# Loading w in pairs of k tiles and storing the last column group in two DMAs: a 64-row window matmul on one core

## The chip, the cores and the metric

One core of a Trainium2 chip runs the whole program. The metric is device time in microseconds (us): the median over several executions. The span that a trace shows, from its first to its last instruction, is 1.6 to 1.7 us shorter than the time of the same execution (184.73 against 183.1 before), so differences of spans can be read as differences of time.

## The reference

For each of four batches, 64 consecutive rows of x, from an offset known only at run time, are multiplied by the same w.

```python
B, S, D, W = 4, 4096, 4096, 64
for b in range(B):
    o = int(offsets[b])
    results.append(x[b, o:o+W] @ w)      # (64 x 4096) @ (4096 x 4096), fp32
```

w is 64 MB of fp32 and is used once. x contributes 4 MB, the output is another 4 MB. What counts is how fast w comes in.

## The kernel before

The PE (TensorE) does the matmuls; it adds up its results in banks of PSUM, from which ScalarE and VectorE copy them. Two batches share a tile of 128 rows (G = 2 such tiles). The columns are worked in two groups of 2048 (NG), the k dimension in 32 tiles of 128. Eight PSUM banks hold one column group for both row tiles. A load reads one k tile of one column group, 128 rows of 8 KB (1 MB of fp32), and the DMA casts it to fp16. Only the last k tile of the last group is loaded in four parts, so that its matmuls, copies and stores can follow each other in small steps.

```python
wh_pool = ctx.enter_context(tc.tile_pool(name="wh", bufs=24))
sth_pool = ctx.enter_context(tc.tile_pool(name="sth", bufs=8))
# ... (other pools, the first k tile through ScalarE's queue) ...
def load(ng, ki):
    t = wh_pool.tile([P, NG], fp16, name="wh", tag="wh")
    nc.gpsimd.dma_start(
        out=t[:], in_=w[ki * P : (ki + 1) * P, ng * NG : (ng + 1) * NG])
    return t[:]
# ... (x loaded and transposed) ...
for ng in range(n_ng):
    for ki in range(n_k):
        # ...
        if ng == n_ng - 1 and ki == n_k - 1:
            for j in range(n_sub):                  # four parts of 512 columns
                # ... wl{j} <- 128 rows of 2 KB
        else:
            wh[(ng, ki)] = load(ng, ki)
# ... (matmuls; group 0 is copied to stage[g]) ...
for g in range(G):                                  # group 0: two stores of 1 MB
    nc.gpsimd.dma_start(out=out[2*g : 2*g+2, :, 0:NG], in_=stage[g][:])
ki = n_k - 1
q = [nc.scalar, nc.sync]
for j in range(n_sub):                              # group 1: eight stores of 256 KB
    cs = (n_ng - 1) * NG + j * NT
    for g in range(G):
        mm(g, j, ki, wlast[j][:], False, True)
        s = sth_pool.tile([P, NT], fp32, name="sth", tag="sth")
        # ... copy bank -> s, ScalarE for g == 0, VectorE for g == 1
        q[g].dma_start(out=out[2*g : 2*g+2, :, cs : cs + NT], in_=s[:])
```

In this program a DMA issued from GpSimd gets one of eight semaphores in turn; so does a DMA issued from ScalarE or SyncE, from eight others. A semaphore is a counter that the DMA raises when it has landed. A DMA waits until the one eight places before it has landed.

Of the kernel before, what the change touches and what calls it, by code (L numbers as in the profile page):

```python
# [1 line left out]

# [5 lines left out]


@with_exitstack  # L10
def kernel(
    ctx: ExitStack,
    tc: tile.TileContext,
    x: bass.AP,
    w: bass.AP,
    offsets: bass.AP,
    out: bass.AP,
):
    nc = tc.nc
    fp32 = mybir.dt.float32  # L20
    fp16 = mybir.dt.float16

    B, S, D = x.shape
    _, N = w.shape
    WIN = out.shape[1]
    P = 128
    NT = 512
    NG = 2048
    n_k = D // P
    n_ng = N // NG  # L30
    n_sub = NG // NT
    G = B // 2

    POOL = mybir.EngineType.Pool

    const_pool = ctx.enter_context(tc.tile_pool(name="const", bufs=1))
    x_pool = ctx.enter_context(tc.tile_pool(name="xp", bufs=1))
    wh_pool = ctx.enter_context(tc.tile_pool(name="wh", bufs=24))
    wl_pool = ctx.enter_context(tc.tile_pool(name="wl", bufs=1))
    st_pool = ctx.enter_context(tc.tile_pool(name="st", bufs=1))  # L40
    sth_pool = ctx.enter_context(tc.tile_pool(name="sth", bufs=8))
    psum_pool = ctx.enter_context(tc.tile_pool(name="ps", bufs=1, space=bass.MemoryType.PSUM))

    identity = const_pool.tile([P, P], fp16, name="identity")
    off_t = const_pool.tile([1, B], mybir.dt.int64, name="off_t")
    w0_32 = x_pool.tile([P, N], fp32, name="w0row")
    w0_16 = x_pool.tile([P, N], fp16, name="w0half")
    x16 = [x_pool.tile([P, D], fp16, name=f"xrow{g}") for g in range(G)]
    xT = [x_pool.tile([P, D], fp16, name=f"xT{g}") for g in range(G)]
    ps = [psum_pool.tile([P, NT], fp32, name=f"bank{t}") for t in range(8)]  # L50

    ctx.enter_context(tc.manual_schedule())

    nc.sync.dma_start(out=off_t[:], in_=offsets[None, :])
    nc.scalar.dma_start(out=w0_32[:], in_=w[0:P, :])
    off_i32 = off_t.bitcast(mybir.dt.int32)

    def load(ng, ki):
        t = wh_pool.tile([P, NG], fp16, name="wh", tag="wh")
        nc.gpsimd.dma_start(  # L60
            out=t[:], in_=w[ki * P : (ki + 1) * P, ng * NG : (ng + 1) * NG]
        )
        return t[:]

    wh = {(ng, 0): w0_16[:, ng * NG : (ng + 1) * NG] for ng in range(n_ng)}
    wh[(0, 1)] = load(0, 1)
    make_identity(nc, identity[:])
    for b in range(B):
        g, m = divmod(b, 2)
        o = nc.values_load(  # L70
            off_i32[0:1, 2 * b : 2 * b + 1],
            engines=[POOL],
            min_val=0,
            max_val=S - WIN,
            skip_runtime_bounds_check_because="offsets are drawn below S - WIN",
        )
        nc.gpsimd.dma_start(  # L77
            out=x16[g][m * WIN : (m + 1) * WIN, :],
            in_=x[b][bass.ds(o, WIN), :]
        )  # L80
    wlast = []
    for ng in range(n_ng):
        for ki in range(n_k):
            if (ng, ki) in wh:
                continue
            if ng == n_ng - 1 and ki == n_k - 1:
                for j in range(n_sub):
                    cs = ng * NG + j * NT
                    t = wl_pool.tile([P, NT], fp16, name=f"wl{j}")
                    nc.gpsimd.dma_start(  # L90
                        out=t[:], in_=w[ki * P : (ki + 1) * P, cs : cs + NT]
                    )
                    wlast.append(t)
            else:
                wh[(ng, ki)] = load(ng, ki)

    nc.scalar.copy(out=w0_16[:, :NG], in_=w0_32[:, :NG])  # L97
    nc.scalar.copy(out=w0_16[:, NG:], in_=w0_32[:, NG:])  # L98
    for g in range(G):
        for t in range(8):  # L100
            for i in range(4):
                k = 4 * t + i
                nc.tensor.matmul(  # L103
                    out=ps[t][:, i * P : (i + 1) * P],
                    lhsT=x16[g][:, k * P : (k + 1) * P],
                    rhs=identity[:],
                    start=True,
                    stop=True,
                )
            dst = xT[g][:, t * NT : (t + 1) * NT]  # L110
            if t % 2 == 0:
                nc.vector.tensor_copy(out=dst, in_=ps[t][:])  # L112
            else:
                nc.scalar.copy(out=dst, in_=ps[t][:])  # L114

    def mm(g, j, ki, rhs, start, stop):
        nc.tensor.matmul(  # L117
            out=ps[4 * g + j][:],
            lhsT=xT[g][:, ki * P : (ki + 1) * P],
            rhs=rhs,  # L120
            start=start,
            stop=stop,
        )

    stage = [st_pool.tile([P, NG], fp32, name=f"stage{g}") for g in range(G)]
    for ng in range(n_ng):
        last = ng == n_ng - 1
        for ki in range(n_k - 1 if last else n_k):
            for g in range(G):
                for j in range(n_sub):  # L130
                    mm(g, j, ki, wh[(ng, ki)][:, j * NT : (j + 1) * NT], ki == 0, ki == n_k - 1)
        if not last:
            for j in range(n_sub):
                for g in range(G):
                    dst = stage[g][:, j * NT : (j + 1) * NT]
                    if g == 0:
                        nc.scalar.copy(out=dst, in_=ps[4 * g + j][:])  # L137
                    else:
                        nc.vector.tensor_copy(out=dst, in_=ps[4 * g + j][:])  # L139
    for g in range(G):  # L140
        nc.gpsimd.dma_start(out=out[2 * g : 2 * g + 2, :, 0:NG], in_=stage[g][:])  # L141
    ki = n_k - 1
    q = [nc.scalar, nc.sync]
    for j in range(n_sub):
        cs = (n_ng - 1) * NG + j * NT
        for g in range(G):
            mm(g, j, ki, wlast[j][:], False, True)
            s = sth_pool.tile([P, NT], fp32, name="sth", tag="sth")
            if g == 0:
                nc.scalar.copy(out=s[:], in_=ps[4 * g + j][:])  # L150
            else:
                nc.vector.tensor_copy(out=s[:], in_=ps[4 * g + j][:])  # L152
            q[g].dma_start(out=out[2 * g : 2 * g + 2, :, cs : cs + NT], in_=s[:])  # L153


# [1 line left out]
_INS = ['x', 'w', 'offsets']  # L157
_OUTS = [((4, 64, 4096), 'float32')]


# [23 lines left out]
```

## Time and profile before

| | before |
|---|---|
| time | 184.98 us (184.97 to 185.01, 3 runs) |
| span of the trace | 183.1 us |
| PE busy | 126.3 us (69%) |
| GpSimd busy | 38.3 us (21%) |
| DMA engines | full from slice 1 to slice 38 of 40 |

Lines from the page of the kernel before. In the first two, each of 40 entries is a slice of 4.58 us: the busy share of the 16 DMA engines in tenths, and what they moved (GB/s as written, so a casting load counts half of what it reads). Then come the packet counts, the queue of the GpSimd DMAs, the chain of waits by line, the two groups that matter (busy us, mean ns, idle us before it and its main cause), and DMA issues (KB each, median us from issue to landing).

```profile
DMA  6999999999999999999999999999999999999994
GB/s 179 348 221 215 207 213 215 215 214 211 213 211 214 215 213 214 214 216 214 211 214 212 213 213 214 213 215 214 215 213 212 213 214 212 213 213 205 387 403 172
DMA packets 11271, 40.97 MB, mean 224 GB/s; under 512 B 1282, under 2 KB 1794, under 8 KB 10626
...
q0 software_dynamic: 9968, 36.70, 97.0%
...
DMA wh<-in_w_dram 90%; ACT sth L150 1%; PE bank L117 1%; ACTq L153 1%; POOLq L60 0%; POOLq L168 0%
...
L117 PE MATMUL bank<-wh,xT 128*128 128x512 f16 x488 | 113.8, 378 | 28.6 <-DMA wh<-in_w_dram 28.6
...
L60 POOL DMA_DIRECT2D wh<-in_w_dram x61 | 32.4, 531 | 112.5 <-DMA wh<-in_w_dram 100.2
...
wh<-in_w_dram POOLq DMA_DIRECT2D x61, 512.0 KB, 19.1
...
out_dram<-sth ACTq DMA_DIRECT2D x4, 256.0 KB, 6.5
out_dram<-sth SPq DMA_DIRECT2D x4, 256.0 KB, 6.6
```

The DMA row and the chain agree: the kernel is a stream of DMA work, and the PE waits for tiles. 19.1 us from issue to landing is not the length of one load. It is the length of a queue of eight.

The end of the time line of the kernel before (start us, us, engine, line, what, and in brackets the idle time before it and what ended it):

```profile
166.48 1.89 PE L117 MATMUL bank<-wh,xT 128*128 128x512 f16 x8 [0.52 <-DMA wh<-in_w_dram]
...
168.93 1.89 PE L117 MATMUL bank<-wh,xT 128*128 128x512 f16 x8 [0.57 <-DMA wh<-in_w_dram]
...
170.65 1.89 PE L117 MATMUL bank<-wl,xT 128*128 128x512 f16 x8
171.07 0.58 ACT L150 COPY sth<-bank 128x512 f32<-128x512 f32 x1 [73.36 <-PE bank L117]
...
171.69 0.34 ACTq L153 DMA_DIRECT2D out_dram<-sth  x1
172.01 2.12 SPq L153 DMA_DIRECT2D out_dram<-sth  x4
```

A k tile is used every 2.45 us and costs the PE 1.89 us. The DMA's share and rate in windows of that end (the numbers at the end of each line are the granted PE clock, DMA share, GB/s):

```profile
169.00:171.00 2.00, 2.00 (x10) 0.90 (x10) 0.00 (x0) 0.00 (x0) 0.00 (x0) 1.00 1.23 297
...
173.00:175.00 2.00, 0.00 (x0) 0.00 (x0) 0.77 (x2) 1.17 (x2) 0.00 (x0) 0.97 1.01 426
...
177.00:179.00 2.00, 0.00 (x0) 0.00 (x0) 0.00 (x0) 0.00 (x0) 0.00 (x0) 0.50 1.06 410
179.00:181.00 2.00, 0.00 (x0) 0.00 (x0) 0.00 (x0) 0.00 (x0) 0.00 (x0) 0.50 0.75 287
```

The DMA engines stay full until 179 us and more, long after the last matmul: 4 MB of stores follow the loads.

### The profile page before, as it was taken

The numbers are of one execution on the slowest core, as the hardware profiler recorded it, in microseconds if no ns is written. First come the engines' busy times: TensorE is split into PE (matmuls) and PEld (weight loads), VectorE is DVE, ScalarE is ACT, GpSimd is POOL, SyncE is SP. The second block draws the span as 40 slices with busy tenths as digits, with TensorE's granted clock in tenths as the row PEclk, the third lists the DMA queues.
The fourth block names the chain that finished last, engine by engine and source line by source line (L and its number), as shares of the span: only waits on it lengthen the run. The fifth ranks groups of instructions, "written<-read, shape, count | busy, mean of one in ns | idle before, by whom it ended". The sixth has DMA issues, their size and how long they took to land.

```text
span 183.1 us, 1380 instructions
## 1 busy us (share of the span) xinstructions
PE 126.3 (69%) x576; PEld 56.4 (31%) x576; DVE 10.5 (6%) x16; ACT 14.1 (8%) x19; POOL 38.3 (21%) x77
## 2 busy tenths in 40 slices
PE   0004799988877777887779878777777877777600
PEld 0004664433333233333324333323232333333200
DVE  0002530000000000000005000000000000000500
ACT  2081430000000000000013000000000000000310
POOL 4612221222222112222221222222122222210000
PEclk9999999999999999999999999999999999999965
DMA  6999999999999999999999999999999999999994
GB/s 179 348 221 215 207 213 215 215 214 211 213 211 214 215 213 214 214 216 214 211 214 212 213 213 214 213 215 214 215 213 212 213 214 212 213 213 205 387 403 172
DMA packets 11271, 40.97 MB, mean 224 GB/s; under 512 B 1282, under 2 KB 1794, under 8 KB 10626
## 3 DMA queue, kind: packets, MB, share of 16 engines
q0 software_dynamic: 9968, 36.70, 97.0%
q10 hardware_dynamic: 720, 3.15, 4.7%
q1 hardware_dynamic: 578, 1.05, 1.5%
q8 instruction: 4, 0.07, 0.1%
q14 instruction: 1, 0.01, 0.0%
HBM read 71.30 MB, written 4.19 MB: 412 GB/s over the span
## 4 chain that ended last, share of the span: by engine, by line
DMA 90%; issue 2%; ACT 1%; PE 1%; ACTq 1%; POOLq 0%
DMA wh<-in_w_dram 90%; ACT sth L150 1%; PE bank L117 1%; ACTq L153 1%; POOLq L60 0%; POOLq L168 0%
## 5 line engine op out<-in xcount | busy, mean ns | idle before, releaser
L117 PE MATMUL bank<-wh,xT 128*128 128x512 f16 x488 | 113.8, 378 | 28.6 <-DMA wh<-in_w_dram 28.6
L117 PEld LDWEIGHTS <-xT 128*128 128x128 f16 x512 | 49.8, 97 | 98.0 <-issue 44.1
L60 POOL DMA_DIRECT2D wh<-in_w_dram x61 | 32.4, 531 | 112.5 <-DMA wh<-in_w_dram 100.2
L103 PE MATMUL bank<-identity,xrow 128*128 128x128 f16 x64 | 7.1, 311 | 17.4 <-DMA xrow<-in_x_dram 17.4
L103 PEld LDWEIGHTS <-xrow 128*128 128x128 f16 x64 | 6.7, 147 | 17.6 <-issue 17.6
L150 ACT COPY sth<-bank 128x512 f32<-128x512 f32 x4 | 2.3, 586 | 74.6 <-PE bank L117 73.8
L137 ACT COPY stage<-bank 128x512 f32<-128x512 f32 x4 | 2.1, 600 | 70.5 <-PE bank L117 70.5
L112 DVE CAST xT<-bank 128x512 f16<-128x512 f32 x8 | 5.5, 691 | 19.3 <-PE bank L103 19.3
L152 DVE COPY sth<-bank 128x512 f32<-128x512 f32 x4 | 2.5, 683 | 72.3 <-PE bank L117 72.3
L139 DVE COPY stage<-bank 128x512 f32<-128x512 f32 x4 | 2.5, 682 | 71.7 <-PE bank L117 71.7
L114 ACT CAST xT<-bank 128x512 f16<-128x512 f32 x8 | 4.7, 586 | 6.9 <-PE bank L103 6.9
L117 PE MATMUL bank<-w0half,xT 128*128 128x512 f16 x16 | 4.3, 390 | 0.2 <-DVE stage L139 0.2
L90 POOL DMA_DIRECT2D wl<-in_w_dram x4 | 2.1, 527 | 7.5 <-DMA wh<-in_w_dram 7.5
L77 POOL DMA_DIRECT2D xrow<-in_x_dram x4 | 2.1, 520 | 2.2 <-issue 2.2
L97 ACT CAST w0half<-w0row 128x2048 f16<-128x2048 f32 x1 | 1.9, 1897 | 7.4 <-DMA w0row<-in_w_dram 7.4
L141 POOL DMA_DIRECT2D out_dram<-stage x2 | 1.1, 534 | 4.2 <-DMA wh<-in_w_dram 4.2
L98 ACT CAST w0half<-w0row 128x2048 f16<-128x2048 f32 x1 | 1.9, 1893 | 0.0
L117 PE MATMUL bank<-wl,xT 128*128 128x512 f16 x8 | 1.9, 379 | 0.0
L97 ACT ACT_TABLE_LOAD x1 | 1.3, 1283 | 1.3 <-PEq L168 1.3
masks.py:199 POOL TENSOR_SCALAR_AFFINE_SELECT identity<-identity 128x128 f16<-128x128 f16 x1 | 0.3, 287 | 0.1
masks.py:197 POOL MEMSET identity<- 128x128 f16 x1 | 0.2, 223 | 0.0
L168 POOL MEMSET const-float32-0.0<- 128x1 f32 x1 | 0.1, 98 | 0.4 <-issue 0.4
(3 smaller groups left out, 0.3 us busy)
## 6 DMA issues: line engine op xcount, KB each, us to landing
wh<-in_w_dram POOLq DMA_DIRECT2D x61, 512.0 KB, 19.1
w0row<-in_w_dram ACTq DMA_DIRECT2D x1, 2048.0 KB, 9.0
xrow<-in_x_dram POOLq DMA_DIRECT2D x4, 512.0 KB, 12.3
out_dram<-stage POOLq DMA_DIRECT2D x2, 1024.0 KB, 12.1
out_dram<-sth ACTq DMA_DIRECT2D x4, 256.0 KB, 6.5
out_dram<-sth SPq DMA_DIRECT2D x4, 256.0 KB, 6.6
wl<-in_w_dram POOLq DMA_DIRECT2D x4, 128.0 KB, 14.9
off_t<-in_offsets_dram SPq DMA_DIRECT2D x1, 0.0 KB
```

Source lines behind the costliest of these rows:

```text
L60: nc.gpsimd.dma_start(out=t[:], in_=w[ki * P : (ki + 1) * P, ng * NG : (ng + 1) * NG])
L77: nc.gpsimd.dma_start(out=x16[g][m * WIN : (m + 1) * WIN, :], in_=x[b][bass.ds(o, WIN), :])
L90: nc.gpsimd.dma_start(out=t[:], in_=w[ki * P : (ki + 1) * P, cs : cs + NT])
L97: nc.scalar.copy(out=w0_16[:, :NG], in_=w0_32[:, :NG])
L103: nc.tensor.matmul(out=ps[t][:, i * P : (i + 1) * P], lhsT=x16[g][:, k * P : (k + 1) * P], rhs=identity[:], start=True, stop=True,)
L112: nc.vector.tensor_copy(out=dst, in_=ps[t][:])
L114: nc.scalar.copy(out=dst, in_=ps[t][:])
L117: nc.tensor.matmul(out=ps[4 * g + j][:], lhsT=xT[g][:, ki * P : (ki + 1) * P], rhs=rhs, start=start, stop=stop,)
L137: nc.scalar.copy(out=dst, in_=ps[4 * g + j][:])
L139: nc.vector.tensor_copy(out=dst, in_=ps[4 * g + j][:])
L150: nc.scalar.copy(out=s[:], in_=ps[4 * g + j][:])
L152: nc.vector.tensor_copy(out=s[:], in_=ps[4 * g + j][:])
```

## The change

The intent is fewer, larger DMAs. Two k tiles come with one load of 2 MB, except for single tiles at the ends of the column groups; the pool has 12 buffers of 8 KB per partition for 24 of 4 KB. The last k tile is one load again, and the last column group is stored like the first, in two DMAs of 1 MB with rows of 8 KB.

```diff
-    wh_pool = ctx.enter_context(tc.tile_pool(name="wh", bufs=24))
+    wh_pool = ctx.enter_context(tc.tile_pool(name="wh", bufs=12))
@@ (cut)
-    def load(ng, ki):
-        t = wh_pool.tile([P, NG], fp16, name="wh", tag="wh")
+    def load(ng, ki, n):
+        t = wh_pool.tile([P, n * NG], fp16, name="wh", tag="wh")
         nc.gpsimd.dma_start(
-            out=t[:], in_=w[ki * P : (ki + 1) * P, ng * NG : (ng + 1) * NG]
+            out=t[:].rearrange("p (t n) -> p t n", t=n),
+            in_=w[ki * P : (ki + n) * P, ng * NG : (ng + 1) * NG].rearrange(
+                "(t p) n -> p t n", p=P
+            ),
         )
@@ (cut: the four loads of the last k tile go)
+            if (ng, ki) not in wh:
+                load(ng, ki, 2 if ki < n_k - 4 - (ki % 2) else 1)
@@ (cut: the last group is worked and copied like the first)
-            q[g].dma_start(out=out[2 * g : 2 * g + 2, :, cs : cs + NT], in_=s[:])
+            (q[g] if last else nc.gpsimd).dma_start(
+                out=out[2 * g : 2 * g + 2, :, ng * NG : (ng + 1) * NG],
+                in_=stage[ng][g][:],
+            )
```

More of the change, by code (lines that the diff above doesn't have):

```diff
@@ L37 @@
     x_pool = ctx.enter_context(tc.tile_pool(name="xp", bufs=1))
-    wh_pool = ctx.enter_context(tc.tile_pool(name="wh", bufs=24))
-    wl_pool = ctx.enter_context(tc.tile_pool(name="wl", bufs=1))
+    wh_pool = ctx.enter_context(tc.tile_pool(name="wh", bufs=12))
     st_pool = ctx.enter_context(tc.tile_pool(name="st", bufs=1))
-    sth_pool = ctx.enter_context(tc.tile_pool(name="sth", bufs=8))
     psum_pool = ctx.enter_context(tc.tile_pool(name="ps", bufs=1, space=bass.MemoryType.PSUM))
@@ L56 @@
     off_i32 = off_t.bitcast(mybir.dt.int32)
-    def load(ng, ki):
-        t = wh_pool.tile([P, NG], fp16, name="wh", tag="wh")
+    def load(ng, ki, n):
+        t = wh_pool.tile([P, n * NG], fp16, name="wh", tag="wh")
         nc.gpsimd.dma_start(
-            out=t[:], in_=w[ki * P : (ki + 1) * P, ng * NG : (ng + 1) * NG]
-        )
-        return t[:]
+            out=t[:].rearrange("p (t n) -> p t n", t=n),
+            in_=w[ki * P : (ki + n) * P, ng * NG : (ng + 1) * NG].rearrange(
+                "(t p) n -> p t n", p=P
+            ),
+        )
+        for i in range(n):
+            wh[(ng, ki + i)] = t[:, i * NG : (i + 1) * NG]
     wh = {(ng, 0): w0_16[:, ng * NG : (ng + 1) * NG] for ng in range(n_ng)}
-    wh[(0, 1)] = load(0, 1)
+    load(0, 1, 1)
     make_identity(nc, identity[:])
@@ L80 @@
         )
-    wlast = []
     for ng in range(n_ng):
         for ki in range(n_k):
-            if (ng, ki) in wh:
-                continue
-            if ng == n_ng - 1 and ki == n_k - 1:
-                for j in range(n_sub):
-                    cs = ng * NG + j * NT
-                    t = wl_pool.tile([P, NT], fp16, name=f"wl{j}")
-                    nc.gpsimd.dma_start(
-                        out=t[:], in_=w[ki * P : (ki + 1) * P, cs : cs + NT]
-                    )
-                    wlast.append(t)
-            else:
-                wh[(ng, ki)] = load(ng, ki)
+            if (ng, ki) not in wh:
+                load(ng, ki, 2 if ki < n_k - 4 - (ki % 2) else 1)
     nc.scalar.copy(out=w0_16[:, :NG], in_=w0_32[:, :NG])
@@ L123, in mm @@
         )
-    stage = [st_pool.tile([P, NG], fp32, name=f"stage{g}") for g in range(G)]
+    stage = [
+        [st_pool.tile([P, NG], fp32, name=f"stage{ng}{g}") for g in range(G)]
+        for ng in range(n_ng)
+    ]
+    q = [nc.scalar, nc.sync]
     for ng in range(n_ng):
         last = ng == n_ng - 1
-        for ki in range(n_k - 1 if last else n_k):
+        for ki in range(n_k):
             for g in range(G):
@@ L131 @@
                     mm(g, j, ki, wh[(ng, ki)][:, j * NT : (j + 1) * NT], ki == 0, ki == n_k - 1)
-        if not last:
-            for j in range(n_sub):
-                for g in range(G):
-                    dst = stage[g][:, j * NT : (j + 1) * NT]
-                    if g == 0:
-                        nc.scalar.copy(out=dst, in_=ps[4 * g + j][:])
-                    else:
-                        nc.vector.tensor_copy(out=dst, in_=ps[4 * g + j][:])
-    for g in range(G):
-        nc.gpsimd.dma_start(out=out[2 * g : 2 * g + 2, :, 0:NG], in_=stage[g][:])
-    ki = n_k - 1
-    q = [nc.scalar, nc.sync]
-    for j in range(n_sub):
-        cs = (n_ng - 1) * NG + j * NT
-        for g in range(G):
-            mm(g, j, ki, wlast[j][:], False, True)
-            s = sth_pool.tile([P, NT], fp32, name="sth", tag="sth")
-            if g == 0:
-                nc.scalar.copy(out=s[:], in_=ps[4 * g + j][:])
-            else:
-                nc.vector.tensor_copy(out=s[:], in_=ps[4 * g + j][:])
-            q[g].dma_start(out=out[2 * g : 2 * g + 2, :, cs : cs + NT], in_=s[:])
+        for j in range(n_sub):
+            for g in range(G):
+                dst = stage[ng][g][:, j * NT : (j + 1) * NT]
+                if g == 0:
+                    nc.scalar.copy(out=dst, in_=ps[4 * g + j][:])
+                else:
+                    nc.vector.tensor_copy(out=dst, in_=ps[4 * g + j][:])
+        for g in range(G):
+            (q[g] if last else nc.gpsimd).dma_start(
+                out=out[2 * g : 2 * g + 2, :, ng * NG : (ng + 1) * NG],
+                in_=stage[ng][g][:],
+            )
 _INS = ['x', 'w', 'offsets']
```

## The prediction

> **What bounds the kernel now.** The DMA engines. In the page's 40 slices the DMA row reads 9 from slice 1 to 38; the chain of waits is 90% loads of w; the PE waits 51 times for a w tile (28.6 us). In the time line the last ten k tiles start their matmuls 2.458 us apart, 1 MB of fp32 each: 427 GB/s. The PE needs 1.89 us per tile, so it is not the limit.
>
> By the trace's packet records (40 to 140 us), an engine takes eight rows of 8 KB per load: the next row starts 304 to 305 ns after the last, and 324 ns where a load's completion packet lies between. 7 x 304.9 + 324 = 2458 ns. So one more DMA in a full queue costs about 20 ns, not its latency. The Trainium skill ("DMA: Bandwidth & Descriptors", "Measured") gives 1 MB DMAs 341 GB/s, 16 MB ones 425. This trace disagrees with 341 for a stream: eight loads are always queued (19.1 us from issue to landing), so the fixed cost is hidden already.
>
> **The change, costed.**
> 1. 52 loads of w become 26. Estimate: 26 x 20 ns = 0.52 us less on every engine, on the critical path.
> 2. The last k tile, before in four loads: 2 KB rows 79 ns apart, 32 per engine = 2.53 us plus three completions; as one load 8 x 305 = 2.44 us. Saves 0.15 us; the overlap of the parts with matmuls and copies is lost.
> 3. The eight stores of 2 KB rows: two queues alternate, 160 ns per pair of rows, so 64 rows per engine = 5.12 us, plus completions. As 8 KB rows, like the first group's stores (306 ns apart): 16 x 306 = 4.90 us. Saves 0.3 us.
> Sum: 1.0 us.
> 4. Added: a half's copies must all end before its store is issued. The last tile is usable near 170.9 us of the span. As at the first group's end (copies done 2.5 and 3.8 us after the last tile's matmuls began), stores are issued near 173.4 (ScalarE) and 174.7 (SyncE). First packet about 1.0 us later (the load from ScalarE's queue: issued 0.87, first packet 1.88): 174.4 and 175.7. But the first group's 2 MB of stores lie queued right behind the last load and keep the engines busy until 174 (fastest) to 175.4 (slowest); then the first half takes 2.45 us. So no hole on the slowest engine, at most 0.4 us on the fastest. Before, too, the small stores waited: issued 171.7, first packet 174.75.
>
> Buffers hold as much as before (12 x 8 KB per partition); a 2 MB issue may take POOL 2 x 0.53 us; harmless.
>
> **Prediction: 184.0 us, range 183.2 to 185.0** (before 184.98). Faster by over 2%: 0.02; within 2%: 0.96; slower by over 2%: 0.02.
>
> **What would show it.** Pairs landing near 4.9 us apart, rows still 305 ns apart, first group's stores starting 0.6 to 0.7 us earlier; DMA full until about 1 us before 181.3, without a slower slice; last stores issued near 173.4 and 174.7.
>
> **What would make it wrong.** (a) Rows 2 MB apart in HBM are read slower: each ns on 305 costs 0.4 us (416 rows). (b) A hole between first-group and last-group stores: up to 1 us slower. (c) One engine lags (ends of the loads spread over 1.3 us); the slowest sets the time; another packet order could shift it by half a us. (d) A DMA costs more than 20 ns: up to 2 us faster.

## More of the kernel before

At the end of the program SyncE waits for all semaphores of the DMAs, one instruction after the other. From the view of one source line, the closing sequence on SyncE (first and last start, us, after the durations):

```profile
L179 SPq DRAIN  x3: 7/7/7, 182.2 to 182.5; - x3
```

The first of these drains starts when SyncE has passed its last wait.

## The result, and the profile after

| | before | after |
|---|---|---|
| time, median | 185.0 us (4 runs) | 183.56 us (183.43 to 183.63, 4 runs) |
| ratio to before, 95% interval | | 0.9921 (0.9903 to 0.9938) |
| span of the trace | 183.1 us | 182.0 us |
| PE busy | 126.3 us | 122.8 us |
| GpSimd busy | 38.3 us | 27.7 us |
| DMA packets | 11271 | 9559 |

A ratio is the mean time of one kernel's fast runs over that of the other's of the same rounds, so it is not quite the ratio of the medians. The change saves 1.44 us, 0.8%; the prediction was 1.0 us.

The lines of the page after that answer to those shown of before:

```profile
DMA  5999999999999999999999999999999999999995
GB/s 180 348 217 216 206 214 215 216 214 215 212 213 212 216 215 216 214 215 210 212 214 217 215 215 214 212 214 213 215 216 214 215 215 211 214 212 216 367 398 216
DMA packets 9559, 40.97 MB, mean 225 GB/s; under 512 B 722, under 2 KB 722, under 8 KB 8658
...
q0 software_dynamic: 9120, 36.70, 97.0%
...
DMA wh<-in_w_dram 88%; DVE stage L133 1%; POOL wh L58 1%; PE bank L108 1%; POOLq L72 1%; POOL xrow L79 0%; DVEq L164 0%; POOL identity masks.py:197 0%; POOLq L79 0%; POOLq L58 0%; POOLq masks.py:199 0%; POOLq L153 0%
...
L108 PE MATMUL bank<-wh,xT 128*128 128x512 f16 x496 | 112.0, 379 | 32.7 <-DMA wh<-in_w_dram 32.7
...
L58 POOL DMA_DIRECT2D wh<-in_w_dram x36 | 23.8, 662 | 116.8 <-DMA wh<-in_w_dram 105.8
...
wh<-in_w_dram POOLq DMA_DIRECT2D x26, 1024.0 KB, 36.6
...
out_dram<-stage ACTq DMA_DIRECT2D x1, 1024.0 KB, 4.9
out_dram<-stage SPq DMA_DIRECT2D x1, 1024.0 KB, 6.0
```

The picture is the same: full DMA engines, a waiting PE, the same bytes, 1712 packets fewer. Of these, 560 are small ones, almost all completions (those under 512 B fell from 1282 to 722; a DMA has 16, one on each engine); 384 are rows of the last k tile (512 quarter rows became 128), and 768 are rows of the last stores (1024 became 256). GpSimd issues loads for 23.8 us where it took 32.4, and nobody waited for that.

The time line of the end:

```profile
168.84 1.89 PE L108 MATMUL bank<-wh,xT 128*128 128x512 f16 x8 [0.55 <-DMA wh<-in_w_dram]
...
171.26 1.89 PE L108 MATMUL bank<-wh,xT 128*128 128x512 f16 x8 [0.54 <-DMA wh<-in_w_dram]
...
171.68 2.05 ACT L131 COPY stage<-bank 128x512 f32<-128x512 f32 x4 [73.82 <-PE bank L108]
172.54 2.48 DVE L133 COPY stage<-bank 128x512 f32<-128x512 f32 x4 [73.39 <-PE bank L108]
173.76 0.35 ACTq L135 DMA_DIRECT2D out_dram<-stage  x1
175.05 0.38 SPq L135 DMA_DIRECT2D out_dram<-stage  x1
```

The copies are now done before the first store of the last group is issued, 2.1 us later than before. The windows of the end:

```profile
169.00:171.00 2.00, 1.73 (x8) 0.68 (x7) 0.00 (x0) 0.00 (x0) 0.00 (x0) 1.00 1.07 369
...
173.00:175.00 2.00, 0.15 (x1) 0.00 (x0) 2.00 (x4) 0.73 (x2) 0.00 (x0) 1.00 0.93 393
...
177.00:179.00 2.00, 0.00 (x0) 0.00 (x0) 0.00 (x0) 0.00 (x0) 0.00 (x0) 0.77 0.98 410
179.00:181.00 2.00, 0.00 (x0) 0.00 (x0) 0.00 (x0) 0.00 (x0) 0.00 (x0) 0.50 0.40 168
```

The stores of the first group start earlier (369 GB/s against 297 in the first window), there is a shallow hole between 173 and 175 us (0.93 against 1.01), and the work is over earlier (0.40 against 0.75 in the last window). The closing sequence:

```profile
L164 SPq DRAIN  x3: 7/7/7, 181.2 to 181.5; - x3
```

It starts 1.0 us earlier. What follows takes that second apart.

### The profile page after: what moved, and what is told of

It is laid out like the page before. It is cut to its first block, busy times and chain, and to the rows that moved or that the text cites. A ratio compares the mean times of both kernels' runs of the same rounds, so it can differ in the third digit from the quotient of the medians.

```text
span 182.0 us, 1329 instructions
## 1 busy us (share of the span) xinstructions
PE 122.8 (67%) x576; PEld 56.5 (31%) x576; DVE 10.5 (6%) x16; ACT 13.8 (8%) x19; POOL 27.7 (15%) x48
## 2 busy tenths in 40 slices
DMA packets 9559, 40.97 MB, mean 225 GB/s; under 512 B 722, under 2 KB 722, under 8 KB 8658
## 4 chain that ended last, share of the span: by engine, by line
DMA 88%; issue 3%; POOL 1%; DVE 1%; POOLq 1%; PE 1%; DVEq 0%
DMA wh<-in_w_dram 88%; DVE stage L133 1%; POOL wh L58 1%; PE bank L108 1%; POOLq L72 1%; POOL xrow L79 0%; DVEq L164 0%; POOL identity masks.py:197 0%; POOLq L79 0%; POOLq L58 0%; POOLq masks.py:199 0%; POOLq L153 0%
## 5 line engine op out<-in xcount | busy, mean ns | idle before, releaser
L108 PE MATMUL bank<-wh,xT 128*128 128x512 f16 x496 | 112.0, 379 | 32.7 <-DMA wh<-in_w_dram 32.7
L58 POOL DMA_DIRECT2D wh<-in_w_dram x36 | 23.8, 662 | 116.8 <-DMA wh<-in_w_dram 105.8
L131 ACT COPY stage<-bank 128x512 f32<-128x512 f32 x8 | 4.1, 599 | 144.4 <-PE bank L108 144.4
L133 DVE COPY stage<-bank 128x512 f32<-128x512 f32 x8 | 5.0, 682 | 145.1 <-PE bank L108 145.1
```

The lines of the kernel that those rows point to most:

```text
L58: nc.gpsimd.dma_start(out=t[:].rearrange("p (t n) -> p t n", t=n), in_=w[ki * P : (ki + n) * P, ng * NG : (ng + 1) * NG].rearrange("(t p) ...
L108: nc.tensor.matmul(out=ps[4 * g + j][:], lhsT=xT[g][:, ki * P : (ki + 1) * P], rhs=rhs, start=start, stop=stop,)
L131: nc.scalar.copy(out=dst, in_=ps[4 * g + j][:])
L133: nc.vector.tensor_copy(out=dst, in_=ps[4 * g + j][:])
```

## The experiments

All kernels gave the correct result. Theory A throughout is this: the DMA engines' work falls by an amount that can be counted from the packets, and what the clock shows of it is decided by the slowest engine and by what comes after its last packet. The rivals are named in the expectations. The table at the end of this section uses the packet records and the landing times of the traces. A DMA has landed on an engine when that engine's update of the semaphore arrives; the lag, below, is how far the slowest of the 16 engines is behind their mean at the landing of the last load of w.

### The changed kernel again

There is no edit.

> The changed kernel once more, as the control on this chip. Theory A (DMA work falls by a counted amount, and the slowest engine and the final waits decide how much of it shows): ratio to before again 0.992, about 1.4 us less (1.1 to 1.7). In its first profile the mean landing of the first group's last store came 0.77 us earlier than before, the slowest engine's only 0.86, and from the last landing to the last wait's end it took 0.08 us instead of 0.45. I expect the last two to repeat, and the slowest engine's lag behind the mean at the end of the loads (1.1 us, before 0.77) to move by up to 0.3 us, since it was set in the start-up. Rival B (it is chance of the chip that ran it): ratio within 0.3% of 1.

Measured: 183.53 us (183.44 to 183.71), before 184.96 us on the same chip, ratio 0.9922 (0.9908 to 0.9936). Rival B, chance of one chip, falls: this was chip 15, and a later run on chip 14 gave 0.9924. The lag of the slowest engine at the end of the loads was 0.94 us instead of 1.11, and the 0.08 us from the last landing to the end of the waits repeated.

### Only the pairs

```diff
 (to the kernel before)
-    wh_pool = ... bufs=24
+    wh_pool = ... bufs=12
-                wh[(ng, ki)] = load(ng, ki)
+                load(ng, ki, 2 if ki < n_k - 4 - (ki % 2) else 1)
```

> Only the loads of w are paired (26 merges); last k tile in four loads, eight small stores as before. Theory A: each merge saves the 20 ns seen between rows where a completion packet lies, 0.52 us in the mean over engines, so the first group's stores start 0.5 us earlier in the mean; time 0.3 to 0.8 us less than before, depending on the slowest engine's lag. The final waits stay as before (0.4 us after the last landing). Rival C (a DMA costs a larger fixed part than the packets show): 1.0 us or more of the 1.4 comes from here alone. Rival D (rows 2 MB apart are read slower): row spacing above 305 ns and a time no better than before.

Measured: 184.50 us against 184.96, ratio 0.9972 (0.9958 to 0.9985). The first group's store packets start at 172.18 us in the mean, against 172.72 and 172.74 in two traces of before: 0.55 us for 26 merges, 21 ns each. The row spacing says the same: in a stretch without an instruction fetch (107 to 141 us) a load of 1 MB takes 2.458 us on an engine and a pair 4.895 us, 20 ns less than two. Theory A holds, in the mean over engines and in time (0.46 us). Rival C wanted 1.0 us or more from the pairs alone, rival D no gain; both fall. About a third of the whole gain comes from the part of the change that its title puts first.

### Only the end

```diff
 (to the changed kernel)
-    wh_pool = ... bufs=12
+    wh_pool = ... bufs=24
-                load(ng, ki, 2 if ki < n_k - 4 - (ki % 2) else 1)
+                load(ng, ki, 1)
```

> Only the end is changed: last k tile as one load, one store of 1 MB for each half; w loads of 1 MB as before. Theory A: no gain in the loads but 0.1 to 0.15 us at the last tile; stores 0.1 to 0.3 us; 0.37 us because the last store now has the last semaphore in the closing sequence of waits, instead of one with six waits behind it; together 0.6 to 0.9 us less than before. Rival C: less than 0.4 us.

Measured: 183.89 us against 184.96, ratio 0.9944 (0.9930 to 0.9958). That is 1.07 us, above the 0.6 to 0.9 expected and far above rival C's 0.4. Together with the pairs it makes 1.53 us; the whole change gave 1.43 on the same chip. Within the intervals the two parts add up. In this trace the last data packet ends at 180.88 us (before 181.29 and 181.51), and the rest of the gain comes after it, as the table below shows: 0.37 us of waits, which the expectation had, and 0.16 us between the last data packet and the landing, which it had not.

### Before, with the closing waits in another order

The eight semaphores of ScalarE's and SyncE's DMAs are handed out in turn. Before, the loads of the offsets and of the first k tile take the first two, the eight stores take the other six and then the first two again. The closing sequence waits for them in a fixed order. So when the store that lands last lets it go on, six waits for stores that have landed already are still to come. Six more tiny loads shift the assignment by six.

```diff
 (to the kernel before)
+    pad = [const_pool.tile([1, B], mybir.dt.int64, name=f"pad{i}") for i in range(6)]
     ...
+    for t in pad:
+        nc.sync.dma_start(out=t[:], in_=offsets[None, :])
```

> The kernel before with nothing changed in its work, but six loads of 32 bytes added at the very start on SyncE's queue, so that the eight small stores take the eight semaphores in order and the two last stores end on the last two that the closing sequence waits for. Theory A: the waits after the last landing shrink from 0.45 us to under 0.15 us, and the time falls by 0.3 to 0.4 us, although six DMAs were added. Rival E (the closing waits are not on the path, the final drain takes as long anyway): time within 0.1 us of before, or longer.

Measured: 184.63 us against 184.96, ratio 0.9982 (0.9969 to 0.9996). Adding six DMAs made the kernel before 0.33 us faster. In its trace, the view of the closing line reads:

```profile
L182 SPq DRAIN  x3: 7/7/7, 182.1 to 182.4; - x3
```

The last landing in this trace was at 182.02 us and the drain follows 0.08 us later. Before it was 0.45 us later. Rival E falls.

### After, with the closing waits in the old order

```diff
 (to the changed kernel: the same six loads)
+    for t in pad:
+        nc.sync.dma_start(out=t[:], in_=offsets[None, :])
```

> The changed kernel with the six 32-byte loads added at the start, so that its two last stores get the first two semaphores of the closing sequence again, with six waits behind them. The mirror of the run in which the kernel before got the last ones. Theory A: 0.3 to 0.4 us slower than the changed kernel (183.53), near 183.9, with about 0.45 us from the last landing to the end of the waits. Rival E: within 0.1 us of 183.53.

Measured: 183.87 us, ratio 0.9941 (0.9927 to 0.9955), against 0.9922 for the changed kernel in its own rounds: 0.34 us slower. This run and the changed kernel's were on two chips, and the intervals of their ratios overlap; but the five times here (183.72 to 183.93) lie above all fourteen of the changed kernel (183.34 to 183.71), and the trace below shows where the time goes. The same six loads speed up one kernel and slow down the other, by the same amount.

```profile
L167 SPq DRAIN  x3: 7/7/7, 181.3 to 181.6; - x3
```

Here the last landing was at 180.87 us, and the drain comes 0.45 us after it.

### Four k tiles to a load

```diff
 (to the changed kernel)
-    wh_pool = ... bufs=12
+    wh_pool = ... bufs=6
-                load(ng, ki, 2 if ki < n_k - 4 - (ki % 2) else 1)
+                load(ng, ki, 4 if ki < n_k - 7 else 2 if ki < n_k - 5 else 1)
```

> The changed kernel with four k tiles (4 MB) to a load where it had two: 12 loads of four and 2 of two instead of 26 of two, six buffers of 16 KB. 12 completions less. Theory A (20 ns each): the first group's stores start 0.24 us earlier in the mean over engines than in the changed kernel (mean packet start near 171.8 us), time 0.1 to 0.4 us less than the changed kernel's 183.53, near 183.3. Rival C (larger DMAs are worth more than their completion packets): 0.6 us or more. Rival F (deeper queue or fewer buffers cost something): slower than 183.5.

Measured: 183.37 us (183.19 to 183.94), ratio 0.9920 (0.9906 to 0.9934). The first group's stores start at 171.91 us in the mean, 0.14 to 0.21 us earlier than in the three traces of the changed kernel: 12 to 18 ns for each of the 12 merges. In a stretch without a fetch a load of four tiles takes 9.777 us, two pairs 9.791: 14 ns, not 20. The PE is nearer to the path here. With six buffers GpSimd waits 135.7 us in all for the PE to free one, the granted clock was 0.93 to 0.94 (0.97 to 0.99 in all other runs), and the chain of waits gives the PE 23%, where it had 1%; the DMA engines stay full all the same. In time this run decided nothing, so both kernels were run again on one chip.

> The kernel with four k tiles to a load once more, on the same chip as the changed kernel of the next run, since their first runs were on two chips and 0.16 us apart. Theory A, corrected by the first run (first group's stores 0.14 to 0.18 us earlier in the mean over engines, not 0.24): 0.05 to 0.25 us less than the changed kernel. Rival F (nothing is left to gain from larger loads): within 0.05 us of it, or slower.

> The changed kernel a third time, for the comparison with four k tiles to a load: 183.5 us, ratio to before 0.992. Its trace gives one more lag of the slowest engine at the end of the loads: between 0.8 and 1.15 us if the lag is set afresh in each execution (so far 1.11 and 0.94 for this kernel).

Measured: four tiles 183.33 us (183.23 to 183.39, 4 runs), ratio 0.9911 (0.9896 to 0.9927); two tiles 183.57 us (183.34 to 183.64), ratio 0.9924 (0.9910 to 0.9937). The means are 0.19 us apart, in the expected direction and of the expected size, but the intervals overlap. Four tiles to a load is probably a little better than the changed kernel and has not been shown to be. The lag of the third trace of the changed kernel was 0.82 us, inside the range told.

### The last stores in halves

```diff
 (to the changed kernel)
+                if last and j % 2 == 1:
+                    lo, hi = (j - 1) * NT, (j + 1) * NT
+                    q[g].dma_start(
+                        out=out[2 * g : 2 * g + 2, :, ng * NG + lo : ng * NG + hi],
+                        in_=stage[ng][g][:, lo:hi])
```

> The changed kernel with each of its two last stores cut in two (512 KB, rows of 4 KB), issued as soon as two of the four copies are done, so about 1.0 us earlier for the first. Theory A: the hole on the fast engines (DMA share 0.93 between 173 and 175 us) closes, but the slowest engine had no hole, so the time moves by less than 0.15 us either way. Rival G (the wait for all four copies costs time on the path): 0.2 us or more faster than 183.53.

Measured: 183.55 us, ratio 0.9924 (0.9911 to 0.9938), the same as the changed kernel's 0.9922. The first half store was issued at 172.62 us instead of about 173.6. The hole closed, as expected (a DMA share of 0.99 between 173 and 175 us, where it was 0.93), and nothing came of it. The wait for four copies is off the path, as predicted; rival G falls.

### More instruction fetches

The trace shows four DMAs of 16 KB on the instruction queue, each about 0.9 us on one DMA engine.

```diff
 (to the changed kernel)
-        nc.tensor.matmul(out=ps[4 * g + j][:], lhsT=..., rhs=rhs, start=start, stop=stop)
+        h = NT if start or stop else NT // 2
+        for c in range(0, NT, h):
+            nc.tensor.matmul(out=ps[4 * g + j][:, c : c + h], lhsT=...,
+                             rhs=rhs[:, c : c + h], start=start, stop=stop)
```

> The changed kernel with the matmuls of all k tiles but the first and last of a group cut in two of 256 columns: about 960 more PE instructions, so about twice the 16 KB instruction fetches (4 of about 0.93 us in the trace, each on one DMA engine), and the same DMA work otherwise; the PE should stay under the 2.45 us of a load. Theory A (the slowest engine's lag of 1.0 to 1.1 us is set by these fetches, which hold one engine at a time): 7 to 9 fetches, the mean over engines later by 16 KB/16 each, that is 0.2 to 0.3 us in all, the slowest engine's lag larger by up to 0.9 us if a fetch falls on an engine that is behind already; time 0.2 to 1.2 us longer than 183.53. Rival H (the lag has another cause, the start-up alone): lag and time unchanged within 0.15 us.

Measured: 183.62 us (183.37 to 183.71), ratio 0.9930 (0.9916 to 0.9943). The page counts eight fetches where the changed kernel has four:

```profile
q8 instruction: 8, 0.13, 0.3%
```

The last load of w lands at 170.32 us in the mean over engines, 0.17 to 0.24 us later than in three traces of the changed kernel (170.08 to 170.15): the expected cost in the mean, nearly (0.2 to 0.3). But the slowest engine finishes at 170.97 us, exactly as early as there (170.97 to 171.22), so the lag fell to 0.66 us instead of growing, and the time hardly moved: 0.09 us above 183.53, where at least 0.2 was expected. Half of my theory of the lag falls; rival H was right about the time. In the landings of single loads one sees one engine drop back at each fetch (for example at the first, in the changed kernel's first trace: the largest distance from the mean goes from 0.35 to 1.90 us within one load, then settles near 1.3). At the second fetch of the same trace another engine falls back, to 0.93 us. So fetches do make stragglers; but more of them hit other engines, fill up the gap between the mean and the slowest, and leave the end where it was: with eight fetches, nine of the 16 engines end the loads between 0.01 and 0.66 us behind the mean.

### Before again

There is no edit; one look, no state.

> The kernel before, one look for a second trace: 184.9 to 185.1 us; lag of the slowest engine at the end of the loads 0.75 to 1.0 us (0.77 in its first trace, 0.96 with the six tiny loads added); seven waits of 0.06 us still after the last landing, 0.4 to 0.5 us.

Measured: 184.95 us, lag 0.97 us, 0.45 us of waits after the last landing. As expected. This trace is nearer to the median time of before than the first one, whose execution was a quick one (184.73 us), so the sums below are made with it.

### The end of each trace, taken apart

All in us of the span, worked out from packet records, landing times and SyncE's closing instructions. "Loads, mean" and "loads, slowest" are the landing of the last load of w in the mean over the 16 engines and on the slowest. "Waits left" counts the waits of the closing sequence that end after the last landing, that for the last store included.

| kernel | loads, mean | loads, slowest | last data packet ends | last landing | first drain | waits left | span |
|---|---|---|---|---|---|---|---|
| before, first trace | 170.72 | 171.50 | 181.29 | 181.78 | 182.23 | 7 | 183.08 |
| before again | 170.75 | 171.72 | 181.51 | 182.01 | 182.45 | 7 | 183.30 |
| only the pairs | 170.21 | 171.29 | 181.00 | 181.51 | 181.95 | 7 | 182.81 |
| before, other order of waits | 170.81 | 171.77 | 181.57 | 182.02 | 182.10 | 1 | 182.95 |
| only the end | 170.64 | 171.44 | 180.88 | 181.22 | 181.30 | 1 | 182.12 |
| after, first trace | 170.12 | 171.22 | 180.75 | 181.09 | 181.17 | 1 | 181.99 |
| after again | 170.08 | 171.02 | 180.55 | 180.89 | 180.97 | 1 | 181.79 |
| after, third time | 170.15 | 170.97 | 180.51 | 180.85 | 180.93 | 1 | 181.75 |
| after, old order of waits | 170.16 | 171.00 | 180.53 | 180.87 | 181.32 | 7 | 182.17 |

From "before again" to "after, third time", whose times (184.95 and 183.4) lie near the two medians, the difference of 1.55 us is: 1.00 us until the last data packet, 0.16 us from there to the landing (0.50 against 0.34), 0.36 us of waits (0.44 against 0.08), 0.03 us after. The last three, 0.55 us in all, come out the same for every trace of the two kernels. The first, until the last data packet, does not: this pair gives the largest of the six differences between the two traces of before and the three of the changed kernel, which run from 0.54 to 1.00 us. With 1.44 us between the medians, 0.89 us is left for it.

The table also shows that it is the slowest engine that decides. From its last landing of w to the last data packet it takes 9.79 us in both traces of before and 9.53 to 9.54 us in the three of the changed kernel (9.71 us with only the pairs, 9.44 with only the end). The spread of the first difference is therefore mostly that of the lag.

## Why the prediction was right or wrong

**What bounds the kernel: right.** The DMA engines were full before and after, and the PE's extra waiting (32.7 us instead of 28.6) cost nothing. The Trainium skill ("DMA: Bandwidth & Descriptors", "Rules for kernel authors") asks for 1 MiB or more per DMA. Here the loads read that much already, with eight in the queue, and doubling it gave 0.25% (0.46 us). The page does not say how much is left above that size; in this full queue it was little.

**Term 1, the merges: right.** Predicted 0.52 us, measured 0.55 us in the mean over engines and 0.46 us in time, by the run that had nothing else. Going on to four tiles gave about 14 ns for each merge, so the figure of 20 ns should not be carried far.

**Terms 2 and 3, the last tile and the larger rows of the stores: right in sum.** Predicted 0.45 us. The run with only the end changed has its last data packet 0.41 us earlier than the first trace of before, 0.63 us earlier than the second; the lag of the first was 0.77 us and of the second 0.97, and 0.79 in the run, so the first is the fairer comparison. Apart, term 2 is smaller than told: with only the end changed, the last load of w lands 0.08 to 0.11 us earlier in the mean, not 0.15. Term 3 is near the 0.3 told: the stretch from the slowest engine's last load to the last data packet is 0.26 us shorter in the changed kernel than in before (9.53 against 9.79), and 0.35 with only the end changed.

**The sum of 1.0 us: right for the data, within the spread of the traces.** From "before again" to "after, third time" the last data packet moves by 1.00 us, but that exact agreement is luck, since it is the largest of six; 0.89 us is what fits the two medians. With the first traces it is only 0.54, because the first execution of before had the small lag of 0.77 us and the first of after the large one of 1.11. The prediction named this as (c). In the traces of before the lag at the end of the loads is 0.77 and 0.97, in those of the changed kernel 0.82, 0.94 and 1.11: the ranges overlap, and no effect of the pairs on it is shown. The range of 183.2 to 185.0 us was wide; its upper end was the time of before, so by itself it said little.

**Term 4, the copies: right.** The stores were issued at 173.5 to 173.8 and 174.8 to 175.05 us, 0.1 to 0.4 us later than told. The hole shows as 0.93 in a window of 2 us. Issuing earlier changed nothing, so it lies on the fast engines, off the path.

**What would be seen: right except for one item.** Pairs land 4.895 us apart in a stretch without a fetch (near 4.9 told), and the spacing of rows inside a load keeps its peak at 304 to 305 ns, so fear (a) did not come true. "Without a slower slice" does not hold for the window of the hole.

**The step that was missing.** The prediction's sum ended with the last packet: "DMA full until about 1 us before 181.3", and from there it took the rest as unchanged. It is not. Two terms were left out. Together they measure 0.52 us, which covers the 0.44 us by which the change beat the prediction. The first is 0.36 us of closing waits: with ten DMAs on the two hardware queues, the last two stores reused the first two semaphores of a sequence that takes about 60 ns for each entry; with four DMAs, the last store has the last one. Both mirror runs show it (0.33 us gained, 0.34 us lost, by the same six tiny loads), and it has nothing to do with the size of the DMAs, only with how many there are before the last. The second is 0.16 us between the last data packet and its landing: 0.44 to 0.51 us in the four traces that end with 2 KB rows, 0.34 in the five of the table that end with 8 KB rows. In the first trace of before, the last completion packet (the small packet with which an engine ends its part of a DMA) is over 0.01 us after the last data packet, so the extra time lies between that packet and the landing. The run with half stores narrows it down: four stores with 4 KB rows took 0.33 us, so rows shorter than 8 KB alone don't make it. Whether 2 KB rows or eight stores in flight do was not tested; that stays open.

## What to carry to other kernels

When a stream of DMAs is kept full, price one DMA more or less by the gap between packets in the trace (here about 20 ns from 1 MB to 2 MB, 14 ns from 2 MB to 4 MB), not by its latency alone or by its time from issue to landing. When fewer DMAs make a kernel faster by more than the data explains, look behind the last packet: the semaphore that the last store happens to get decides how many closing waits come after it. And when the difference looked for is under half a percent, take more than one trace of each kernel, because the slowest of 16 engines lags by a different amount each time.

## What the Trainium skill lacked or had wrong

- "DMA: Bandwidth & Descriptors", "Measured": it gives 341 GB/s for a DMA of 1 MB and does not say whether others were queued with it; the 6.15 us in the same row would make about 170. A queue of eight casting loads of 1 MB ran at 427 GB/s here (1 MB of fp32 in 2.458 us). The page lacks the cost of one more DMA in a full queue: 20 to 21 ns on each engine at 1 MB (0.55 us for 26 merges), about 14 ns at 2 MB.
- The same page, "Anatomy of one DMA", which is about DMAs issued from GpSimd, calls the bubble of a completion write about one cycle and the cost of setup and completion together constant, about 2.0 us. Here a completion packet between two rows of such a load widened their spacing from 305 to about 325 ns, 20 ns. And the part from the last data packet to the landing was not constant: for the first group's stores, which GpSimd issues, it was 0.34 to 0.35 us in the traces of the changed kernel and 0.51 to 0.52 in those of before, where the small stores ran beside them. For the last stores, from ScalarE and SyncE, it was 0.34 us with 8 KB rows and 0.44 to 0.51 us for eight stores with 2 KB rows.
- No page has the closing sequence: after the last landing, waits on semaphores already reached still cost about 60 ns each, in a fixed order (0.45 us with seven left, 0.08 us with one). "Runtime: NRT & Kernel Launch", "The ~15µs preamble/postamble breakdown", has a wait for all engines after the kernel, with no cost for each semaphore that the program itself waits for.
- "Runtime: NRT & Kernel Launch", "Instruction fetch mechanics", calls the cost of crossing a 16 KiB boundary of the instructions one tail-bump of a DMA queue, "mostly hidden". In this kernel, which is bound by DMA, a fetch takes 0.89 to 0.98 us of one DMA engine: four more of them moved the last load by 0.17 to 0.24 us in the mean over engines, though not its slowest engine.
